# A two-layer hybrid backbone with product-key experts: 320 dense tokens in place of 384 in the first layer, the second context tile's gathers put last

## The chip, the cores and the metric

The kernel runs on one core of a Trainium2 chip. The time is the device time of one execution in microseconds, the median over several runs.

## The reference

Two layers over 512 latent tokens and 256 context tokens of width 1024. Each layer mixes tokens by three head groups and then sends every token through PEER, a product-key expert layer with 16384 one-neuron experts; 8 heads pick 16 experts each, 128 per token:

```python
hx = rmsnorm(x, norm1_g[l]) * (1.0 + sc1) + sh1
hc = rmsnorm(ctx, norm1_g[l]) * (1.0 + csc1) + csh1
yx, yc = token_mixer(hx, hc, need_ctx, ...)
x = x + g1 * yx
x = x + g2 * peer(rmsnorm(x, norm2_g[l]) * (1.0 + sc2) + sh2, ...)
# in peer:
act = gelu(einsum('td,thkd->thk', xb, u_tab[eid]))
return einsum('thk,thkd->td', gate * act, v_tab[eid])
```

`token_mixer` projects by `w_in` and runs a bidirectional RG-LRU (context first, its last states start the latents'), latent attention over context and latent keys, and a Hyena convolution (FFT) on the latents. The context is updated in layer 0 only; in layer 1 it still feeds the LRU and the attention. The output is the normalized latent stream.

## The kernel before, in words

Everything is in float32; where it pays, an operand is split into two float32r parts and multiplied in three passes (`mm`, `split`, `load_split`). The instructions are laid out by a tile framework at build time: under `prio(level)` a lower number goes first on each engine, and each engine then runs its queue in order. `schedule` (L173) sets the levels: the context's layer 0 first, the latents' layer 0 at 3, the dense experts at 3 (layer 1: 5), the gathers at 6, that is, wherever nothing else is ready.

Experts are computed in two ways. **Dense** (`peer_x`): T tokens go through all 16384 experts. 128 u-blocks of `peer_u` are split and multiplied with the tokens (`ublock`, tile `pst`), GELU goes into a ring of nA + nB slots (tiles `PA`, `PB`); `weights` builds each token's gates by comparing indices with an iota (`o`, `og`, matmuls `pwt`, L1231), eight tokens a unit, in three chunks of the 128 blocks, and multiplies them into the ring; `vblock` multiplies the slots with a v-block into PSUM (`dacc`). Every vn-th v-block is left unsplit and multiplied as plain float32. The last half tile of 64 tokens, where T has one, is always plain (L1254). The loop's order is written out: at step m the due weight units, v-block m, u-block m + R, R = nA + nB. Route (the top-16 choice) runs ahead of it beside the first nA u-blocks.

**Gathered** (`gtile_u`, `gtile_v`): for each of a tile's 128 choices an indirect DMA on the GpSimd queue (`rows_of`, L1089) fetches one table row per token, 128 rows of 4 KB, into one of five `grow` buffers; VectorE multiplies it with the tokens and sums (u, L1100) or adds it weighted to `acc` (v, L1113). A half tile (H) holds both halves of its choices side by side and needs 64 gathers of u and 64 of v. Full tiles are G, dense ones D.

Before the change, layer 0 gathers both context tiles (gc[0], gc[1]) and the latents' fourth tile (gx[3]): three times 128 of u and 128 of v, in the order gc[0] u and v, gc[1] u, gx[3] u and v, gc[1] v. Layer 1 gathers the fourth tile and half of the third.

`front` (L455 on) is the token mixer's first half: transposes (`transposed`), the `w_in` projections block by block (tile `pwin`), with `post` writing each to its place, through `upad` (padded by two memsets on GpSimd, L499 and L500 or their like) and `conv` where a convolution follows; then Hyena and the LRU (`lru`, matmuls `lpg`, L714). In layer 1 it runs with ctx=True: the blocks 9, 10, 11, 0, 1, 2 also project the context, for which `gtile_v` of gc[1] must have been written to `csd` and reloaded (`xr`, L424). The context's LRU comes ahead of the latents'. `back` holds the attention and the output projection. Pools on the left and right side are stacks: a pool opened later lies where a closed one lay, and its loads wait for it.

```python
for m in range(-nB, 128):
    for c, i in due.get(m, ()):
        weights(c, i, sp)
    if m >= 0:
        vblock(m, sp)
    if nA <= m + R < 128:
        ublock(m + R)
```

Of the kernel before, what the change touches and what calls it, by code (L numbers as in the profile page):

```python
# [9 lines left out]
F32 = mybir.dt.float32  # L10
F32R = mybir.dt.float32r
F16 = mybir.dt.float16
I32 = mybir.dt.int32
# [58 lines left out]
class Kern:  # L72
# [50 lines left out]
    def run(self):  # L123
        tc, nc, a = self.tc, self.nc, self.a
        with ExitStack() as es:
# [15 lines left out]
            nc.scalar.activation(self.scc, self.scc, AF.Silu)  # L141
            self.iota = pp.tile([128, 128], F32, name="iota")
            nc.gpsimd.iota(self.iota, pattern=[[1, 128]], base=0, channel_multiplier=0,
                           allow_small_or_imprecise_dtypes=True)
            self.iotah = pp.tile([128, 128], F16, name="iotah")
            nc.vector.tensor_copy(self.iotah, self.iota)
            self.ranks = pp.tile([128, 16, 8], F16, name="ranks")
            nc.vector.tensor_copy(self.ranks, self.iota[:, 0:16].unsqueeze(2).to_broadcast([128, 16, 8]))
            self.scaled = {}
# [23 lines left out]
    def schedule(self):  # L173
        a = self.a
        with ExitStack() as er:
# [27 lines left out]
            with self.prio(6):  # L203
                self.gtile_u(0, gc[0])
                self.gtile_v(0, 1, 0, gc[0])
                self.gtile_u(0, gc[1])
            with self.prio(3):
                gx, ex = self.peer_x(0, 384, 6, 32, 32, (36, 46, 46), ex)
            with self.prio(6):
                self.gtile_u(0, gx[3])  # L210
                self.gtile_v(0, 0, 3, gx[3])
                self.gtile_v(0, 1, 1, gc[1])
# [8 lines left out]
            with self.prio(5):  # L221
                gx, _ = self.peer_x(1, 320, 0, 32, 46, (44, 42, 42), ex)
            with self.prio(6):
# [230 lines left out]
    def front(self, es, ps, pr, l, s, low, side="left", split=True, ctx=False):  # L454
# [21 lines left out]
        with ExitStack() as es2:  # L476
            hp = es2.enter_context(self.pool("hyc" + tg, side=side))
            hc = [hp.tile([128, L], F32, name=f"hc_{i}") for i in range(6)]
            with self.pool("win" + tg, side=side) as sp:

                def post(st, L, j, p):
                    if j < 3:
                        u = sp.tile([128, LX + 3], F32, name="upad", bufs=2)
                        nc.gpsimd.memset(u[:, 0:2], 0.0)
                        nc.gpsimd.memset(u[:, L + 2:L + 3], 0.0)
                        nc.scalar.copy(u[:, 2:L + 2], p)
                        cw = [self.col(l, "lcw", i * 3 + j) for i in range(4)]
                        self.conv(st["xx"][j], u, L, cw, self.col(l, "lcb", j))
                    elif j < 6:
                        nc.scalar.activation(st["u1"][j - 3], p, AF.Gelu_apprx_tanh)  # L490
                    elif j < 9:
                        nc.scalar.copy(st["cq"][j - 6], p)
                    elif j < 11:
                        nc.scalar.copy(st["ckv"][j - 9], p)
                    elif j == 11:
                        nc.scalar.copy(st["kr"], p[:96])
                    else:
                        u = sp.tile([128, LX + 3], F32, name="upad", bufs=2)
                        nc.gpsimd.memset(u[:, 0:1], 0.0)  # L499
                        nc.gpsimd.memset(u[:, L + 1:L + 2], 0.0)  # L500
                        nc.scalar.copy(u[:, 1:L + 1], p)
                        cw = [self.col(l, "hcw", i * 6 + j - 12) for i in range(3)]
                        self.conv(hc[j - 12], u, L, cw, self.col(l, "hcb", j - 12))

                def parts(name, L):
                    return [sp.tile([128, KD, L], F32R if split else F32, name=f"{name}{i}") for i in range(1 + split)]

                hT = parts("hT", L)
                for _ in self.transposed(sp, ps, l, 0, s, range(L // 128), hT):
                    pass  # L510
                shared = (9, 10, 11, 0, 1, 2)
                order = (3, 4, 5, 6, 7, 8) + shared if ctx else (0, 1, 2, 9, 10, 11, 3, 4, 5, 6, 7, 8)
                for j in (12, 13, 14, 15, 16, 17) + order:
                    if ctx and j == shared[0]:
                        cT = parts("cT", LC)
                        for _ in self.transposed(sp, ps, l, 0, 1, range(2), cT):
                            pass
                    if split:
                        w = self.load_split(sp, "w_in", a["w_in"][l, j], bufs=3, parts=2)
                    else:  # L520
                        raw = sp.tile([128, KD, 128], F32, name="w_in", bufs=2)
                        nc.sync.dma_start(raw, a["w_in"][l, j])
                        w = [(raw[:, k, :],) for k in range(KD)]
                    for n, h, t in ((L, hT, st), (LC, cT, sc)) if ctx and j in shared else ((L, hT, st),):
                        p = ps.w("pwin")[:, :n]
                        for k in range(KD):
                            self.mm([p], [w[k]], [[x[:, k, :] for x in h]], k == 0, k == KD - 1)
                        post(t, n, j, p)
            with self.pool("nrm" + tg, side=side) as sp:
                self.rmsn(sp, ps, l, L, st["ckv"], "kvg", 256)  # L530
                self.rmsn(sp, ps, l, L, st["cq"], "qg", 384)
                with self.prio(low):
                    self.hyena(ps, l, s, hc, st["cat"], side)
        with self.prio(low), ExitStack() as ek:
            if ctx:
                kp = ek.enter_context(self.pool("kvc", side="right"))
                self.lru(pr, l, 1, sc, False, low - 1)
                self.mla(ps, ps, l, 1, sc, False, pool=kp)
            self.lru(pr, l, s, st, True, low - 1)
# [9 lines left out]
    def back(self, ps, pr, l, s, st, ex, mods=()):  # L549
# [6 lines left out]
        with self.pool(f"wo{l}{s}", side="right") as sp, ExitStack() as es2:  # L556
            wo = {}

            def load(pool, ks):

                for k in ks:
                    raw = pool.tile([128, D], F32, name="woraw" if l else f"wo{k}")
                    nc.sync.dma_start(raw, a["w_out"][l, k])
                    wo[k] = [raw]
                    if l:
                        wo[k] = [pool.tile([128, D], F32R, name=f"wo{n}{k}") for n in "hl"]
                        self.split(*wo[k], raw)
# [322 lines left out]
    def route(self, ps, l, s, kinds, hT=None, iT=None, i2n=None, side="left", done=None, fill=iter(())):  # L890
# [8 lines left out]
        with ExitStack() as es:  # L899
# [7 lines left out]
            with self.pool(f"rn{l}{s}", side=side) as sp:  # L907
                A2 = self.load_row(sp, l, 2, s, "A2")
                B2 = self.load_row(sp, l, 1, s, "B2")
                for i, x in enumerate(self.transposed(sp, ps, l, 1, s, range(nt), hT, rest)):  # L910
                    if kinds[i] == "D":
                        continue
                    outs[i] = h = gp.tile([128, D], F32, name="ghx", bufs=2)
                    for dst, src in ((LO, HI), (HI, HI)) if kinds[i] == "H" else ((ALL, ALL),):
                        nc.vector.tensor_mul(h[dst], x[src], A2[src])
                        nc.vector.tensor_add(h[dst], h[dst], B2[dst])
# [5 lines left out]
            sel = [self.sel_tiles(sp, i) for i in range(nt)]  # L922
            eid = {i: gp.tile([128, 128], I32, name="eid", bufs=3) for i in range(nt) if kinds[i] != "D"}
            for h in range(8):
# [167 lines left out]

    def gtile_u(self, l, routed):
        nc = self.nc
        hx, eid, gate, n = routed
        dot = self.gp.tile([128, 128], F32, name="dot")
        junk = self.gp.tile([128, D], F32, name="acc")
        for j in range(n):
            r = self.rows_of("peer_u", eid, j)
            nc.vector.scalar_tensor_tensor(junk, r, 1.0, hx, op0=ALU.mult, op1=ALU.mult, accum_out=dot[:, j:j + 1])  # L1100
        nc.scalar.activation(dot[:, :n], dot[:, :n], AF.Gelu_apprx_tanh)
        nc.vector.tensor_mul(gate[:, :n], gate[:, :n], dot[:, :n])

    def gtile_v(self, l, s, t, routed):
# [25 lines left out]
        if l == 0:  # L1130
            nc.sync.dma_start(self.sd[s][t], res)
            if s == 0:
                nc.sync.dma_start(self.res[0][:, t, :], self.sd[0][t])

# [15 lines left out]
    def peer_x(self, l, T, vn, nA, nB, widths, ex):  # L1150
# [11 lines left out]
        with ExitStack() as es:  # L1162
# [40 lines left out]
            def weights(c, i, sp):  # L1203
# [8 lines left out]
                nc.vector.tensor_tensor(  # L1212
                    paired(o1), paired(self.iotah[:, cuts[c]:cuts[c + 1]].unsqueeze(1)).to_broadcast(bc),
                    tk[:, 0].unsqueeze(2).to_broadcast(bc), op=ALU.is_equal)
# [6 lines left out]
                if i % 2 == 0:  # L1221
                    bc = [128, NC, 64, 2]
                    nc.vector.tensor_tensor(paired(o2), paired(self.iotah.unsqueeze(1)).to_broadcast(bc),
                                            tk[:, 1].unsqueeze(2).to_broadcast(bc), op=ALU.is_equal)
# [206 lines left out]
```

## Time and profile before

| what | value |
| --- | --- |
| median of the runs | 4282.57 us (4280.38 to 4297.57) |
| the profiled execution | 4280.5 us, span 4278.7 us |
| mean granted TensorE clock | 0.937 of 2.4 GHz |
| layer 0: route, dense experts | 905 to 1250, 1250 to 2475 us |
| layer 1: mixer, route, dense experts | 2475 to 2960, 2960 to 3260, 3260 to 4252 us |

The table's stages are read from the timeline; times are from the span's start. A row of the page or of a view names line, engine, operation and tile; xcount is the number of instructions. A busy PE is not PE at its peak, since matmuls overlap and their ends are modelled.

### The profile page before, as it was taken

Reading aid. Unit: us, or ns where it says so; the run is one execution under the profiler, and the core shown is the slowest. Engines: PE = TensorE matmul, PEld = TensorE weight load, DVE = VectorE, ACT = ScalarE, POOL = GpSimd, SP = SyncE. Lnnn points to the kernel's source line nnn. Section 1 sums busy time; section 2 is a strip of 40 time slices with the busy share of each in tenths; the row PEclk is TensorE's granted clock in tenths of the full one; section 3 lists DMA queues with packets and bytes.
Section 4 is the critical chain, followed back from the end, with each engine's and each line's share of the span. In section 5 each row is a group of like instructions: output and inputs, shape, how many; then the busy total and the mean of one; then the engine's idle time right before and its main releaser. Section 6 shows DMA issues by size and latency. Waiting matters only on the chain.

```text
span 4278.7 us, 63806 instructions
## 1 busy us (share of the span) xinstructions
PE 3732.9 (87%) x22530; PEld 2815.8 (66%) x22530; DVE 3506.5 (82%) x7435; ACT 1898.1 (44%) x3715; POOL 1524.6 (36%) x1225
## 2 busy tenths in 40 slices
PE   7887987968989989998868979887889999999997
PEld 3645544548878877877656657446888887776654
DVE  5746987889989988988898874754899998888988
ACT  4454342533247525622462233633325655555732
POOL 0000244652344563366426620000126345553243
PEclk7998997988999999999989989998999999999998
DMA  5554587885768897799879962252359888887697
GB/s 195 199 199 153 202 310 233 280 300 195 243 223 270 309 353 258 236 364 357 287 228 330 353 205 90 70 157 95 117 194 336 284 295 304 291 293 279 225 353 273
DMA packets 305154, 1062.90 MB, mean 248 GB/s; under 512 B 35468, under 2 KB 42336, under 8 KB 304834
## 3 DMA queue, kind: packets, MB, share of 16 engines
q0 software_dynamic: 165888, 604.05, 40.6%
q1 hardware_dynamic: 138946, 454.78, 30.5%
q8 instruction: 177, 2.90, 0.3%
q14 instruction: 143, 1.17, 0.1%
HBM read 1041.85 MB, written 16.84 MB: 247 GB/s over the span
## 4 chain that ended last, share of the span: by engine, by line
PE 33%; DMA 21%; DVE 17%; issue 16%; POOL 7%; ACT 5%; SPq 0%; POOLq 0%; DVEq 0%; ACTq 0%
PE pst L121 7%; POOL grow L1089 7%; DMA grow<-in_peer_u_dram,eid 6%; PE dacc L121 6%; DMA grow<-in_peer_v_dram,eid 5%; PE pwin L121 4%; DMA uv<-in_peer_ut_dram 4%; DMA uv<-in_peer_v_dram 4%; DVE uvl L114 3%; PE ppq L121 3%; DVE acc L1100 2%; DVE acc L1113 2%; DMA wmod<-in_w_mod_dram 2%; PE pwo L121 2%; PE fp L404 1%
## 5 line engine op out<-in xcount | busy, mean ns | idle before, releaser
L1089 POOL DMA_INDIRECT grow<-in_peer_u_dram,eid x576 | 754.0, 1309 | 1144.2 <-DVE acc L1100 562.0
L1089 POOL DMA_INDIRECT grow<-in_peer_v_dram,eid x576 | 762.7, 1324 | 767.3 <-DVE acc L1113 623.8
L121 PE MATMUL pst<-dhT,uvh 128*128 128x384 f32 (+1 forms) x4096 | 997.9, 328 | 0.0
L113 ACT CAST uvh<-uv 128x1024 fp32r<-128x1024 f32 x491 | 513.0, 1045 | 689.6 <-DMA uv<-in_peer_v_dram 414.2
L121 PE MATMUL pst<-dhT,uvl 128*128 128x384 f32 (+1 forms) x2048 | 695.1, 340 | 106.6 <-DVE uvl L114 75.0
L1113 DVE SCALAR_TENSOR_TENSOR acc<-grow,gate,acc 128x1024 f32<-128x1024 f32 x571 | 732.9, 1284 | 52.1 <-DMA grow<-in_peer_v_dram,eid 45.2
L1100 DVE SCALAR_TENSOR_TENSOR acc<-grow,ghx 128x1024 f32<-128x1024 f32 x576 | 704.6, 1223 | 66.7 <-DMA grow<-in_peer_u_dram,eid 61.3
L114 DVE TENSOR_TENSOR uvl<-uv,uvh 128x1024 fp32r<-128x1024 f32 x491 | 599.5, 1223 | 164.5 <-ACT uvh L113 160.5
L121 PEld LDWEIGHTS pst<-dhT,uvh 128*128 128x128 f32 x4096 | 729.8, 192 | 4.2 <-issue 2.2
L121 PEld LDWEIGHTS pst<-dhT,uvl 128*128 128x128 f32 x2048 | 394.3, 193 | 206.4 <-DVE uvl L114 154.8
L121 PE MATMUL dacc<-uvh,wl 128*128 128x512 f32 x1154 | 484.0, 420 | 38.5 <-DVE wl L114 22.3
L121 PE MATMUL dacc<-uvl,wh 128*128 128x512 f32 x1154 | 470.6, 408 | 20.4 <-DVE uvl L114 20.0
L121 PE MATMUL dacc<-uvh,wh 128*128 128x512 f32 x1154 | 466.3, 404 | 0.0
L1227 ACT ACTIVATE o<-iota,di2n 128x128 f16<-128x128 f32 x1056 | 325.5, 390 | 26.2 <-PE pwt L1231 26.0
L121 PEld LDWEIGHTS dacc<-uvh,wl 128*128 128x128 f32 x1154 | 222.3, 193 | 127.0 <-DVE wl L114 29.0
L121 PEld LDWEIGHTS dacc<-uvl,wh 128*128 128x128 f32 x1154 | 223.0, 193 | 79.2 <-DVE uvl L114 34.0
L121 PEld LDWEIGHTS dacc<-uvh,wh 128*128 128x128 f32 x1154 | 222.6, 193 | 48.8
L1231 PEld LDWEIGHTS <-o 128*128 128x128 f16 x4224 | 126.5, 97 | 113.3 <-DVE og L1217 33.4
L1231 PE MATMUL pwt<-og,o 128*128 128x46 f16 (+3 forms) x4224 | 152.5, 183 | 45.1 <-DVE og L1217 36.9
L1197 ACT ACTIVATE PA<-pst 128x384 f32<-128x384 f32 (+1 forms) x128 | 59.5, 464 | 281.7 <-PE pst L121 281.6
L1197 ACT ACTIVATE PB<-pst 128x384 f32<-128x384 f32 (+1 forms) x128 | 59.1, 462 | 222.7 <-PE pst L121 222.2
L254 POOL MEMSET rmod<- 128x512 f32 (+1 forms) x8 | 3.3, 416 | 422.8 <-DMA rows<-rmod 112.8
(398 smaller groups left out, 6122.2 us busy)
## 6 DMA issues: line engine op xcount, KB each, us to landing
uv<-in_peer_ut_dram SPq DMA_DIRECT2D x256, 512.0 KB
uv<-in_peer_v_dram SPq DMA_DIRECT2D x256, 512.0 KB
wmod<-in_w_mod_dram SPq DMA_DIRECT2D x96, 512.0 KB
wpq<-in_peer_wq_dram SPq DMA_DIRECT2D x48, 512.0 KB
w_in<-in_w_in_dram SPq DMA_DIRECT2D x72, 256.0 KB
w_in<-in_w_in_dram SPq DMA_DIRECT2D x18, 512.0 KB
grow<-in_peer_u_dram,eid POOLq DMA_INDIRECT x576, 6.5
grow<-in_peer_v_dram,eid POOLq DMA_INDIRECT x576, 6.7
```

The lines of the kernel that those rows point to most:

```text
L113: self.nc.scalar.copy(hi, src)
L114: self.nc.vector.tensor_tensor(lo, src, hi.bitcast(F32), op=ALU.subtract)
L121: self.nc.tensor.matmul(p, w[i], x[j], start=start and n == 0, stop=stop and n == len(passes) - 1)
L254: nc.gpsimd.memset(r, 0.0)
L404: self.nc.tensor.matmul(p, w, x, start=(i == 0), stop=(i == len(pairs) - 1))
L1089: self.nc.gpsimd.indirect_dma_start(out=r, out_offset=None, in_=self.a[table], in_offset=bass.IndirectOffsetOnAxis(ap=eid[:, j:j + 1], axi ...
L1100: nc.vector.scalar_tensor_tensor(junk, r, 1.0, hx, op0=ALU.mult, op1=ALU.mult, accum_out=dot[:, j:j + 1])
L1113: nc.vector.scalar_tensor_tensor(acc, r, w[:, j:j + 1], acc, op0=ALU.mult, op1=ALU.add)
L1197: nc.scalar.activation(slot(i), p, AF.Gelu_apprx_tanh)
L1227: nc.scalar.activation(o2[:, q], self.iota, AF.Abs, bias=i2n[:, t, k * NC + q:k * NC + q + 1])
L1231: nc.tensor.matmul(p[:, q, :], o2[:, q, :], og[:, g, q, :], start=(g == 0), stop=(g == 1))
```

## The change

In layer 0, 320 latent tokens are dense in place of 384: the third tile becomes H and is gathered too. Every second v-block is plain (vn 6 to 2), and the ring grows from 64 to 75 slots; layer 1's shrinks from 78 to 75. Of gc[1] only the first 32 u gathers stay ahead of the latents' tiles; the other 96 and its 128 v gathers come last. In layer 1's `front`, the context is projected in a `project` call of its own, with its own pool and a second load of six `w_in` blocks, behind Hyena in the order of the code. Smaller parts: the iota is kept in fp16 alone, `upad` is as long as its tile, `woraw` comes from another pool, `ghx` has three buffers, `heid` holds an H tile's indices, `gtile_v` writes the rows that it has.

```diff
             with self.prio(6):
                 self.gtile_u(0, gc[0])
                 self.gtile_v(0, 1, 0, gc[0])
-                self.gtile_u(0, gc[1])
+                self.gtile_u(0, gc[1], 0, 32)
             with self.prio(3):
-                gx, ex = self.peer_x(0, 384, 6, 32, 32, (36, 46, 46), ex)
+                gx, ex = self.peer_x(0, 320, 2, 32, 43, (42, 42, 44), ex)
             with self.prio(6):
-                self.gtile_u(0, gx[3])
-                self.gtile_v(0, 0, 3, gx[3])
+                for i in sorted(gx, reverse=True):
+                    self.gtile_u(0, gx[i])
+                    self.gtile_v(0, 0, i, gx[i])
+                self.gtile_u(0, gc[1], 32, 128)
                 self.gtile_v(0, 1, 1, gc[1])
...
-                gx, _ = self.peer_x(1, 320, 0, 32, 46, (44, 42, 42), ex)
+                gx, _ = self.peer_x(1, 320, 0, 32, 43, (44, 42, 42), ex)
...
-                shared = (9, 10, 11, 0, 1, 2)
-                order = (3, 4, 5, 6, 7, 8) + shared if ctx else (0, 1, 2, 9, 10, 11, 3, 4, 5, 6, 7, 8)
-                for j in (12, 13, 14, 15, 16, 17) + order:
-                    if ctx and j == shared[0]:
-                        cT = parts("cT", LC)
-                        for _ in self.transposed(sp, ps, l, 0, 1, range(2), cT):
-                            pass
+                for j in order:
                     if split:
-                        w = self.load_split(sp, "w_in", a["w_in"][l, j], bufs=3, parts=2)
+                        w = self.load_split(sp, "w_in", a["w_in"][l, j], bufs=bufs, parts=2)
...
-                    for n, h, t in ((L, hT, st), (LC, cT, sc)) if ctx and j in shared else ((L, hT, st),):
-                        p = ps.w("pwin")[:, :n]
-                        for k in range(KD):
-                            self.mm([p], [w[k]], [[x[:, k, :] for x in h]], k == 0, k == KD - 1)
-                        post(t, n, j, p)
+                    p = ps.w("pwin")[:, :L]
+                    for k in range(KD):
+                        self.mm([p], [w[k]], [[x[:, k, :] for x in hT]], k == 0, k == KD - 1)
+                    post(sp, st, L, j, p)
+
+            with self.pool("win" + tg, side=side) as sp:
+                project(sp, st, s, L, (12, 13, 14, 15, 16, 17, 0, 1, 2, 9, 10, 11, 3, 4, 5, 6, 7, 8), 3)
...
             if ctx:
+                with self.pool("winc", side=side) as sp:
+                    project(sp, sc, 1, LC, (0, 1, 2, 9, 10, 11), 3)
                 kp = ek.enter_context(self.pool("kvc", side="right"))
                 self.lru(pr, l, 1, sc, False, low - 1)
...
-    def gtile_u(self, l, routed):
+    def gtile_u(self, l, routed, j0=0, j1=None):
...
-        for j in range(n):
+        for j in range(j0, j1):
```

## Rows read from the trace of the kernel before

**Rows 1.** The page, part 1: busy us (share of span), instructions.

```profile
PE 3732.9 (87%) x22530; PEld 2815.8 (66%) x22530; DVE 3506.5 (82%) x7435; ACT 1898.1 (44%) x3715; POOL 1524.6 (36%) x1225
```

**Rows 2.** Windows by stage: length, busy (count), PE clock, DMA share, GB/s.

```profile
1250.00:2475.00 1225.00, 1100.81 (x6861) 895.98 (x6859) 1086.41 (x1683) 542.71 (x1053) 641.61 (x481) 0.96 0.87 305
2475.00:2707.00 232.00, 187.62 (x834) 146.39 (x834) 149.15 (x282) 98.20 (x200) 20.70 (x40) 0.89 0.37 125
...
3260.00:4252.00 992.00, 937.81 (x6345) 708.75 (x6344) 884.14 (x1370) 516.68 (x992) 450.04 (x330) 0.99 0.86 300
```

**Rows 3.** Windows within layer 0's dense stage; columns as before.

```profile
1440.00:1610.00 170.00, 157.28 (x724) 131.59 (x724) 144.16 (x218) 49.35 (x69) 111.73 (x82) 0.97 0.95 350
1610.00:1790.00 180.00, 171.80 (x1379) 143.22 (x1378) 164.10 (x332) 119.04 (x260) 61.45 (x48) 0.96 0.73 244
1790.00:2070.00 280.00, 256.37 (x1227) 210.87 (x1226) 239.47 (x278) 83.18 (x123) 174.70 (x131) 0.97 0.94 345
```

**Rows 4.** Waits of POOL, 1250 to 2475: us in total, times, longest.

```profile
POOL grow L1089 <- DVE acc L1113: 229.2, 121, 8.9
```

**Rows 5.** Groups by shape, DVE, 1250 to 2475: busy, mean ns.

```profile
L1113 DVE SCALAR_TENSOR_TENSOR acc<-grow,gate,acc 128x1024 f32<-128x1024 f32 x235 | 302.2, 1286 | 24.8 <-DMA grow<-in_peer_v_dram,eid 21.1
L1100 DVE SCALAR_TENSOR_TENSOR acc<-grow,ghx 128x1024 f32<-128x1024 f32 x244 | 298.3, 1223 | 24.0 <-DMA grow<-in_peer_u_dram,eid 21.3
L114 DVE TENSOR_TENSOR uvl<-uv,uvh 128x1024 fp32r<-128x1024 f32 x205 | 250.7, 1223 | 79.1 <-ACT uvh L113 78.3
```

**Rows 6.** Groups by shape, DVE, 3260 to 4252.

```profile
L114 DVE TENSOR_TENSOR wl<-PB,wh 128x256 fp32r<-128x256 f32 x64 | 26.9, 421 | 0.4 <-ACT wh L113 0.4
```

**Rows 7.** Timeline, layer 0's dense stage: start, length, engine, what.

```profile
1526.27 0.33 PE L121 MATMUL pst<-dhT,uvl 128*128 128x384 f32 x1
...
1526.79 0.33 PE L121 MATMUL pst<-dhT,uvl 128*128 128x384 f32 x1
...
2459.63 5.31 PE L121 MATMUL dacc<-uv,PB 128*128 128x512 f32 x12
```

**Rows 8.** Timeline of PE, layer 1's dense stage.

```profile
3562.72 0.57 PE L1231 MATMUL pwt<-og,o 128*128 128x42 f16 x16
...
3563.68 0.39 PE L121 MATMUL dacc<-uvh,wh 128*128 128x512 f32 x1
3563.91 0.39 PE L121 MATMUL dacc<-uvh,wl 128*128 128x512 f32 x1
...
3566.07 1.08 PE L1254 MATMUL dacc<-uv,PA 128*64 128x512 f32 x4
...
3568.05 0.31 PE L121 MATMUL pst<-dhT,uvl 128*128 128x320 f32 x1
...
3568.49 0.31 PE L121 MATMUL pst<-dhT,uvl 128*128 128x320 f32 x1
```

**Rows 9.** DMA, 2475 to 2525: a queue; issues, median us to landing.

```profile
q0 software_dynamic: 2546, 9.25, 55.0%
...
grow<-in_peer_v_dram,eid POOLq DMA_INDIRECT x16, 6.3
```

**Rows 10.** Window before the dense stage, L1089 alone (gathers).

```profile
1176.00:1250.00 74.00, 19.71 (x16) 0.88 0.48 160
```

**Rows 11.** Chain of waits, layer 1's projections: start, length, what.

```profile
2607.99 8.54 PE pwin L121 x48
...
2616.55 5.72 PE pwin L121 x24
```

**Rows 12.** Timeline of the front: last gather, reload, first LRU matmuls.

```profile
2517.06 1.28 DVE L1113 SCALAR_TENSOR_TENSOR acc<-grow,gate,acc 128x1024 f32<-128x1024 f32 x1
...
2526.55 0.42 SPq L424 DMA_DIRECT2D xr<-csd  x1
...
2661.52 1.03 PE L714 MATMUL lpg<-cxx,gw 128*128 128x256 f32 x4
...
2715.63 2.92 PE L714 MATMUL lpg<-xx,gw 128*128 128x512 f32 x6
```

More of the change, by code (lines that the diff above doesn't have):

```diff
@@ L141, in run @@
             nc.scalar.activation(self.scc, self.scc, AF.Silu)
[L142 to L146, printed above, removed]
-            self.ranks = pp.tile([128, 16, 8], F16, name="ranks")
-            nc.vector.tensor_copy(self.ranks, self.iota[:, 0:16].unsqueeze(2).to_broadcast([128, 16, 8]))
+            self.iota = pp.tile([128, 128], F16, name="iota")
+            self.ranks = pp.tile([128, 16, 8], F16, name="ranks")
+            with self.pool("iota") as sp:
+                iota = sp.tile([128, 128], F32, name="iota32")
+                nc.gpsimd.iota(iota, pattern=[[1, 128]], base=0, channel_multiplier=0,
+                               allow_small_or_imprecise_dtypes=True)
+                nc.vector.tensor_copy(self.iota, iota)
+                nc.vector.tensor_copy(self.ranks, iota[:, 0:16].unsqueeze(2).to_broadcast([128, 16, 8]))
             self.scaled = {}
@@ L478, in front @@
             hc = [hp.tile([128, L], F32, name=f"hc_{i}") for i in range(6)]
[L479 to L508, printed above, removed]
@@ new lines, in post @@
+            def post(sp, st, L, j, p):
+                if j < 3:
+                    u = sp.tile([128, L + 3], F32, name="upad", bufs=2)
+                    nc.gpsimd.memset(u[:, 0:2], 0.0)
+                    nc.gpsimd.memset(u[:, L + 2:L + 3], 0.0)
+                    nc.scalar.copy(u[:, 2:L + 2], p)
+                    cw = [self.col(l, "lcw", i * 3 + j) for i in range(4)]
+                    self.conv(st["xx"][j], u, L, cw, self.col(l, "lcb", j))
+                elif j < 6:
+                    nc.scalar.activation(st["u1"][j - 3], p, AF.Gelu_apprx_tanh)
+                elif j < 9:
+                    nc.scalar.copy(st["cq"][j - 6], p)
+                elif j < 11:
+                    nc.scalar.copy(st["ckv"][j - 9], p)
+                elif j == 11:
+                    nc.scalar.copy(st["kr"], p[:96])
+                else:
+                    u = sp.tile([128, L + 3], F32, name="upad", bufs=2)
+                    nc.gpsimd.memset(u[:, 0:1], 0.0)
+                    nc.gpsimd.memset(u[:, L + 1:L + 2], 0.0)
+                    nc.scalar.copy(u[:, 1:L + 1], p)
+                    cw = [self.col(l, "hcw", i * 6 + j - 12) for i in range(3)]
+                    self.conv(hc[j - 12], u, L, cw, self.col(l, "hcb", j - 12))
@@ L509, in front, with project @@
+            def project(sp, st, s, L, order, bufs):
+                hT = [sp.tile([128, KD, L], F32R if split else F32, name=f"hT{i}") for i in range(1 + split)]
                 for _ in self.transposed(sp, ps, l, 0, s, range(L // 128), hT):
                     pass
-                shared = (9, 10, 11, 0, 1, 2)
-                order = (3, 4, 5, 6, 7, 8) + shared if ctx else (0, 1, 2, 9, 10, 11, 3, 4, 5, 6, 7, 8)
-                for j in (12, 13, 14, 15, 16, 17) + order:
-                    if ctx and j == shared[0]:
-                        cT = parts("cT", LC)
-                        for _ in self.transposed(sp, ps, l, 0, 1, range(2), cT):
-                            pass
+                for j in order:
@@ L561, in load @@
                 for k in ks:
-                    raw = pool.tile([128, D], F32, name="woraw" if l else f"wo{k}")
+                    raw = sp.tile([128, D], F32, name="woraw") if l else pool.tile([128, D], F32, name=f"wo{k}")
                     nc.sync.dma_start(raw, a["w_out"][l, k])
@@ L912, in route @@
                         continue
-                    outs[i] = h = gp.tile([128, D], F32, name="ghx", bufs=2)
+                    outs[i] = h = gp.tile([128, D], F32, name="ghx", bufs=3)
                     for dst, src in ((LO, HI), (HI, HI)) if kinds[i] == "H" else ((ALL, ALL),):
@@ L922, in route @@
             sel = [self.sel_tiles(sp, i) for i in range(nt)]
-            eid = {i: gp.tile([128, 128], I32, name="eid", bufs=3) for i in range(nt) if kinds[i] != "D"}
+            eid = {i: gp.tile([128, 128], I32, name="eid", bufs=3) if kinds[i] == "G" else sp.tile([128, 128], I32, name="heid") for i in range(nt) if kinds[i] != "D"}
             for h in range(8):
@@ L1091, in rows_of @@
         return r
-    def gtile_u(self, l, routed):
+    def gtile_u(self, l, routed, j0=0, j1=None):
         nc = self.nc
         hx, eid, gate, n = routed
+        j1 = n if j1 is None else j1
         dot = self.gp.tile([128, 128], F32, name="dot")
         junk = self.gp.tile([128, D], F32, name="acc")
-        for j in range(n):
+        for j in range(j0, j1):
             r = self.rows_of("peer_u", eid, j)
             nc.vector.scalar_tensor_tensor(junk, r, 1.0, hx, op0=ALU.mult, op1=ALU.mult, accum_out=dot[:, j:j + 1])
-        nc.scalar.activation(dot[:, :n], dot[:, :n], AF.Gelu_apprx_tanh)
-        nc.vector.tensor_mul(gate[:, :n], gate[:, :n], dot[:, :n])
+        js = slice(j0, j1)
+        nc.scalar.activation(dot[:, js], dot[:, js], AF.Gelu_apprx_tanh)
+        nc.vector.tensor_mul(gate[:, js], gate[:, js], dot[:, js])
     def gtile_v(self, l, s, t, routed):
@@ L1130, in gtile_v @@
         if l == 0:
-            nc.sync.dma_start(self.sd[s][t], res)
+            nc.sync.dma_start(self.sd[s][t][rows], res[rows])
             if s == 0:
-                nc.sync.dma_start(self.res[0][:, t, :], self.sd[0][t])
+                nc.sync.dma_start(self.res[0][rows, t, :], self.sd[0][t][rows])
     def ended(self, sp, l, s, t, rows, y, old, res, fg=None):
@@ L1212, in weights @@
                 nc.vector.tensor_tensor(
-                    paired(o1), paired(self.iotah[:, cuts[c]:cuts[c + 1]].unsqueeze(1)).to_broadcast(bc),
+                    paired(o1), paired(self.iota[:, cuts[c]:cuts[c + 1]].unsqueeze(1)).to_broadcast(bc),
                     tk[:, 0].unsqueeze(2).to_broadcast(bc), op=ALU.is_equal)
@@ L1222, in weights @@
                     bc = [128, NC, 64, 2]
-                    nc.vector.tensor_tensor(paired(o2), paired(self.iotah.unsqueeze(1)).to_broadcast(bc),
+                    nc.vector.tensor_tensor(paired(o2), paired(self.iota.unsqueeze(1)).to_broadcast(bc),
                                             tk[:, 1].unsqueeze(2).to_broadcast(bc), op=ALU.is_equal)
```

## The prediction, made before the changed kernel ran

> **What bounds the kernel now.** The page's busy times come first: TensorE (PE) 87% of the span, VectorE (DVE) 82%, GpSimd (POOL) 36% [rows 1]; neither of the first two is full, so the answer must come from stages. The windows by stage [rows 2] show the first layer's dense experts from 1250 to 2475 us: PE 1100.8 of 1225, DVE 1086.4, DMA share 0.87 at 305 GB/s. Layer 1's dense stage, which already runs with 320 dense tokens, takes 992 us and looks alike (DMA 0.86, 300 GB/s). The front of layer 1, 2475 to 2707, is different: PE 187.6 of 232, DVE 149, DMA 0.37. So in the dense stages three resources run close to full together, and in the front DVE and DMA stand half idle.
>
> Inside the dense stage two kinds of stretch alternate [rows 3]: where few weight units are due (1440 to 1610, 1790 to 2070), the DMA share is 0.94 to 0.95 at 345 to 350 GB/s, with 82 gathers in 170 us of the first; where they are due (1610 to 1790), DVE is busy 164 of 180 us and only 48 gathers pass. What the gather queue waits for is mostly a `grow` buffer that DVE still holds, 229 us for L1113 [rows 4] and the like for L1100. A gather costs DVE 1.22 us and a short read of the accumulator behind it (u) or 1.29 us (v), so I count 1.29; a split of a weight block costs 1.22 us [rows 5]. Gathers are the lowest priority, so they take what the dense work leaves: 481 in 1225 us.
>
> The change takes dense work away and adds 128 gathers (half a tile, u and v), 896 in place of 768 in the first layer; beyond the first context tile's 256, which go first, 640 in place of 512. Context tile 1, whose last 224 gathers come last, must be finished before layer 1's context projection; that before the context LRU, and that before the latents' LRU. I therefore forecast one time: when the latents' LRU starts (2715.6 now [rows 12]). Everything behind it I take as unchanged, layer 1's own dense stage too: its ring shrinks from 78 to 75 u-blocks, so three u-blocks are made later by one v-step each; nothing to 8 us (one step, 992/128), taken as 0.
>
> **Part 1: the dense stage of layer 0.** PE: a group of three u-matmuls takes 0.52 us with 384 columns [rows 7] and 0.44 with 320 [rows 8]; 96 u-blocks x 8 groups x 0.085 = 65 us less. A split v-matmul takes 0.23 us (1.38 per full tile), a plain one 5.31/12 = 0.44 a record, two records to a matmul, so 1.77 a tile; a half tile costs 1.08 us [rows 7, 8]. Before: 107 split and 21 plain v-blocks of three tiles, 443 + 111 = 554 us. After (every second one plain, two and a half tiles): 64 x 3.84 + 64 x 4.62 = 541. Of the 144 weight units 24 go, at 0.57 us [rows 8]: 14 less. PE busy 1101 - 65 - 13 - 14 = 1009; from the other side, layer 1's 938 plus 64 x 0.78 for plain blocks = 988. I take 998. PE's idle time was 124 us here and 54 in layer 1 [rows 2]; there are fewer splits to wait for than here, but more gathers than there, so I take 76, a little under the middle: a stage of 1074 us, bounds 1052 and 1122, 151 us shorter.
>
> Gathers that fit: DVE's other work in layer 1 is 884 - 330 x 1.29 = 458 us [rows 2, 5]; with 64 fewer uvl and wl (1.22 and 0.42 us [rows 5, 6]) it is 353. At layer 1's DVE share of 0.89 that leaves (956 - 353)/1.29 = 467 gathers. DMA: 224 weight blocks of 0.52 MB pass in the stage; at the stage's own 305 GB/s 401 gathers fit beside them, at the 345 GB/s of a stretch with few weight units (1790 to 2070) [rows 3] 481. I take 440, the middle of these two, and less than DVE allows. The latents' 384 gathers go ahead of the context's tail, and with the 16 u gathers left of gc1's first 32 they are 400 of the 440, so the tiles just make the stage's end. 16 were issued before 1250 [rows 10]; the tail left is 640 - 16 - 440 = 184.
>
> **Part 2: the front.** The six shared blocks no longer project context beside the latents: 8.54 against 5.72 us [rows 11], 17 us less, so 232 becomes 215. Its other DVE work is 149 - 21 x 1.28 = 122 us, about 100 without the context's part. At a DVE share of 0.95, a little over the 0.91 of the fullest stretch in [rows 3], (204 - 100)/1.29 = 81 gathers fit. They slow the Hyena chain by up to one gather per hand-over, and the `upad` memsets now queue on POOL behind gathers that wait for a buffer; both cost nothing while the gather stream ends later than Hyena, and are next in line if it doesn't. The 103 gathers left run alone. In the run-out after 2475 the queue moved 9.25 MB in 50 us at a share of 55%, that is 336 GB/s, 1.56 us a gather; five buffers that land in 6.3 us and are held 1.29 give 1.52 [rows 9]. 103 x 1.56 = 161 us.
>
> The Trainium skill, "DMA: Bandwidth & Descriptors", section "Anatomy of one DMA — SWDGE (gpsimd) path", fits a gpsimd DMA at 2.0 us plus its bytes over 436 GB/s; by it a 512 KB gather would land in an estimated 3.2 us, five buffers would never be the limit, and the tail would run at DVE's pace, the second rival below. The trace's 6.3 us speaks against it.
>
> **Part 3: context behind Hyena.** From the last gather's DVE step to the tile's reload took 8.2 us (2518.3 to 2526.55 [rows 12]). Then a landing as a gather's, 6.3 [rows 9], and norm and transposes, estimated as long again: 13; three LRU projections, 3 x 2.82 = 8.5; convolution 2; the context LRU, estimated at half of the 46 us from its first matmul (2661.5) to the front's end at 2707, in which it took turns with Hyena: 23. Sum 55, bounds 45 and 80, the upper one since PE's clock may have fallen in the wait. The second load and split of six `w_in` blocks (3.1 MB, six gathers' worth, 9 us of DMA; 12 DVE pieces of half a uvl) hides in the wait; if the wait is gone, these 10 or so us are paid.
>
> At no cost: the fp16 iota, the third `ghx` buffer and the new pools of `upad`, `heid` and `woraw` (the same instructions, no new wait seen); the u part cut at 32 (two small operations more, under the gathers); the closing of one more tile (5 DVE pieces of 1.2 us, four gathers' worth, inside the bounds).
>
> **Sum.** 1250 + 1074 + 215 + 161 + 55 = 2755, 39 us later than 2715.6. The profiled execution took 4280.5 us; 4319.5 for it, and the median stands 2 us above: 4322. Break-even is a tail of 159 (465 gathers done by the stage's end); each gather more or less is 1.56 us. With 401 done, +100: 4384. With 467, -3: 4281. A stage length other than 1074 nearly cancels, as gathers go on in it.
>
> **Rivals.**
> 1. Faster: the dense stage fills the gaps that it has now, because the plain v-blocks leave DVE free just when the DMA queues have room. At the 350 GB/s of the best stretch throughout, 717 transfers, 493 of them gathers, pass (DVE at 0.95 would allow (1020 - 353)/1.29 = 517): the tail is 131, 50 x 1.56 = 78 us behind the 81 in the front, 44 us earlier: 4239. It decides from 465 gathers. For: DVE above 0.91 and DMA at 0.95 both occur [rows 3]. Against: never together, in neither layer. 0.30.
> 2. The tail at DVE's pace, 1.29 instead of 1.56: 103 x 1.29 = 133, so 11 later than now: 4294. For: in the dense stage POOL waited for DVE, hardly for a DMA [rows 4]. Against: [rows 9]. 0.15.
> 3. The dense stage holds layer 1's flow, 992/330 = 3.0 us a gather: 358 by its end, 42 latent gathers late (66 us, and layer 1 cannot begin), then a tail of 224 - 81 = 143 (223 us): 167 later, 4450. For: the twin stage shows just that. Against: its 128 split v-blocks took 105 us more of DVE. 0.10.
>
> **The numbers.** The forecast has 0.45; its own range is 4281 to 4384 (400 to 467 gathers), and about 0.08 of its chance lies within 0.5%. 0.5%, some 21 us, is about what a measurement of this kernel can tell from no change. Faster: rival 1 mostly, 0.30. Same: rival 2 and the low part of the forecast, 0.24. Slower: 0.46. The range of 8 in 10 takes in the forecast and most of rivals 1 and 2, and leaves out the third and the lowest part of the first: 4222 to 4390.
>
> **What would show it.** Right: layer 0's dense stage near 1074 us with about 440 gathers; gathers through the whole front and some 160 us on behind Hyena with PE idle; the latents' LRU near 2755. Wrong: DVE or DMA above 0.92 throughout the stage (rival 1); L1113 steps 1.3 us apart behind Hyena (rival 2); PE waiting for the latents' reload at the stage's end (rival 3); or a route, an LRU or a layer-1 dense stage of another length than now, which the sum takes as fixed.

## The result and the profile after

The changed kernel takes 4481.4 us (median of 4 runs, 4467.8 to 4486.1) against 4283.2 for the kernel before on the same chips: a ratio of 1.045 [1.0417, 1.0484]. The profiled execution took 4467.75 us, 187 more than the one of before. That lies 159 us above the forecast and beyond the range.

The windows by stage of the changed kernel (columns as in [rows 2]; the lines are layer 0's dense stage, the front to Hyena's end, the wait behind Hyena, the stretch from the latents' first LRU matmul to the end of the output projection, and layer 1's dense stage):

```profile
1250.00:2448.00 1198.00, 1056.58 (x6159) 687.35 (x6159) 954.63 (x1509) 448.10 (x891) 567.32 (x454) 0.97 0.86 302
2448.00:2676.00 228.00, 176.07 (x655) 126.55 (x653) 203.02 (x330) 63.36 (x124) 116.88 (x107) 0.85 0.83 284
2676.00:2871.00 195.00, 33.35 (x189) 28.54 (x190) 136.67 (x163) 43.32 (x91) 98.51 (x83) 0.57 0.69 239
2871.00:3121.00 250.00, 206.87 (x1103) 115.20 (x1101) 128.45 (x239) 99.30 (x176) 1.52 (x4) 0.89 0.32 104
3450.00:4442.00 992.00, 930.74 (x6272) 697.72 (x6272) 875.12 (x1358) 513.73 (x991) 427.30 (x323) 0.99 0.84 295
```

Against [rows 2]: layer 0's dense stage is 27 us shorter, where 151 were forecast, and now neither PE (0.88) nor VectorE (0.80) nor DMA (0.86) is near full. Layer 1's dense stage is within 6 us of what it was: 937 us from its first weight unit to its end at 4436, 931 before (the window above has the length of [rows 2] and runs 6 us past that end). Behind Hyena PE is busy for 33 of 195 us: 138 of them pass to the last gather (at 2814), 57 from there to the latents' LRU at 2871. That start, 155 us later than before, makes most of the 187; 25 more lie between it and the output projection (203 us, 178 before), 7 behind.

What had taken the dense stage is in the waits of SP, whose queue issues the weight loads. In the changed kernel (L1189 loads a block to be split, L1242 a plain one, L1255 is the half tile's matmul; us in total, times, longest), 1250 to 2448:

```profile
SPq L1242 <- PE dacc L1255: 194.7, 43, 10.1
SPq L1189 <- DVE uvl L114: 193.9, 75, 8.7
SPq L1189 <- PE dacc L1255: 154.2, 71, 5.6
```

And in the kernel before, 1250 to 2475:

```profile
SPq L1188 <- DVE uvl L114: 522.6, 152, 10.5
...
SPq L1188 <- PE dacc L121: 27.4, 18, 4.5
```

Before, a load waited for the subtraction that makes `uvl`, VectorE's last look at the raw block, a while before TensorE multiplies the parts. Now 349 us of the waits are for TensorE: the plain half tile reads the raw block itself, in most blocks at the end of their matmuls, and so does a plain block. The timeline of the changed kernel shows one such turn:

```profile
2210.64 1.07 PE L1255 MATMUL dacc<-uv,PA 128*64 128x512 f32 x2
...
2211.65 3.70 PE L121 MATMUL dacc<-uv,PA 128*128 128x512 f32 x8
2211.75 0.33 SPq L1189 DMA_DIRECT2D uv<-in_peer_v_dram  x1
...
2215.28 1.08 PE L1255 MATMUL dacc<-uv,PA 128*64 128x512 f32 x4
2216.40 0.33 SPq L1242 DMA_DIRECT2D uv<-in_peer_v_dram  x1
...
2219.47 1.04 ACT L113 CAST uvh<-uv 128x1024 fp32r<-128x1024 f32 x1 [8.31 <-DMA uv<-in_peer_v_dram]
2219.49 1.97 PE L1255 MATMUL dacc<-uv,PA 128*64 128x512 f32 x2 [3.13 <-DMA uv<-in_peer_v_dram]
2220.54 1.23 DVE L114 TENSOR_TENSOR uvl<-uv,uvh 128x1024 fp32r<-128x1024 f32 x1 [5.09 <-ACT uvh L113]
...
2221.69 2.60 DVE L1114 SCALAR_TENSOR_TENSOR acc<-grow,gate,acc 128x1024 f32<-128x1024 f32 x2
...
2223.23 1.86 POOL L1087 DMA_INDIRECT grow<-in_peer_v_dram,eid  x1 [5.73 <-DVE acc L1114]
```

The half tile's last matmul ends at 2211.71; 0.04 us later the load into its buffer starts. TensorE works on the other buffer until 2216.36 and then waits 3.1 us for the load. Behind that wait its granted clock is 0.50, the lower of its two levels (2219.49 to 2224.40; 1.00 from 2211.65 to 2216.36). The last lines are what the prediction had not seen: VectorE works through its queue in order, so while it waits 5.1 us for the cast of a block that has not landed, the gathers' steps behind wait too, and with them GpSimd for a `grow` buffer. The stall of the dense loop stalls the gathers. Over the stage, VectorE's waits for the cast are 133 us, where they were 78 [rows 5]:

```profile
L114 DVE TENSOR_TENSOR uvl<-uv,uvh 128x1024 fp32r<-128x1024 f32 x166 | 202.8, 1222 | 141.0 <-ACT uvh L113 132.7 <-issue 7.9
```

The same timeline shows a second cost of the half tile. Its two 512-column halves, issued together, run side by side: the four records at 2215.28 take 1.08 us. In the split blocks at 2210.64 and 2219.47 they are issued apart, and each takes as long as both: 1.07 us, or 1.97 at the lower clock. At 2219.49 the first half starts as the raw block lands, while the split parts are still being made. The half tile is torn like this in 31 of the 64 split blocks of the changed kernel. Its cost in the stage, in the changed kernel and in the one with three raw buffers (the first experiment), where it is whole in every block:

```profile
L1255 PE MATMUL dacc<-uv,PB 128*64 128x512 f32 x252 | 89.9, 630 | 8.3 <-DMA uv<-in_peer_v_dram 8.3
L1255 PE MATMUL dacc<-uv,PA 128*64 128x512 f32 x256 | 87.9, 643 | 9.0 <-DMA uv<-in_peer_v_dram 9.0
...
L1255 PE MATMUL dacc<-uv,PA 128*64 128x512 f32 x256 | 69.0, 618 | 0.0
L1255 PE MATMUL dacc<-uv,PB 128*64 128x512 f32 x256 | 69.0, 618 | 0.0
```

### The profile page after: what moved, and what is told of

Its sections match the earlier page's. It is cut to its first block, busy times and chain, and to the rows that moved or that the text cites. A ratio compares the mean times of both kernels' runs of the same rounds, so it can differ in the third digit from the quotient of the medians.

```text
span 4466.0 us, 62529 instructions
## 1 busy us (share of the span) xinstructions
PE 3693.4 (83%) x21824; PEld 2598.2 (58%) x21824; DVE 3569.7 (80%) x7462; ACT 1798.0 (40%) x3543; POOL 1640.2 (37%) x1353
## 4 chain that ended last, share of the span: by engine, by line
PE 35%; DMA 23%; DVE 17%; issue 13%; ACT 7%; POOL 5%; SPq 0%; DVEq 0%; POOLq 0%; ACTq 0%
PE dacc L121 8%; DMA uv<-in_peer_v_dram 8%; PE pst L121 7%; DMA uv<-in_peer_ut_dram 6%; POOL grow L1087 5%; DMA grow<-in_peer_u_dram,eid 3%; DMA grow<-in_peer_v_dram,eid 3%; PE dacc L1255 3%; DVE uvl L114 3%; PE ppq L121 3%; ACT uvh L113 2%; PE pwin L121 2%; DVE acc L1100 2%; PE pwo L121 2%; DVE acc L1114 2%
## 5 line engine op out<-in xcount | busy, mean ns | idle before, releaser
L121 PE MATMUL pst<-dhT,uvh 128*128 128x320 f32 x4096 | 932.6, 315 | 0.0
L1114 DVE SCALAR_TENSOR_TENSOR acc<-grow,gate,acc 128x1024 f32<-128x1024 f32 x634 | 812.4, 1281 | 75.5 <-DMA grow<-in_peer_v_dram,eid 66.4
L121 PE MATMUL pst<-dhT,uvl 128*128 128x320 f32 x2048 | 669.3, 327 | 104.4 <-DVE uvl L114 76.7
L121 PE MATMUL dacc<-uvh,wl 128*128 128x512 f32 x768 | 319.2, 424 | 52.4 <-ACT uvh L113 41.5
L121 PE MATMUL dacc<-uvl,wh 128*128 128x512 f32 x768 | 315.5, 411 | 22.3 <-DVE uvl L114 21.9
L121 PE MATMUL dacc<-uvh,wh 128*128 128x512 f32 x768 | 307.1, 400 | 0.0
L1228 ACT ACTIVATE o<-iota,di2n 128x128 f16<-128x128 f16 x960 | 296.5, 389 | 24.0 <-PE pwt L1232 20.4
L1255 PE MATMUL dacc<-uv,PA 128*64 128x512 f32 x512 | 163.2, 631 | 13.8 <-DMA uv<-in_peer_v_dram 12.9
L1255 PE MATMUL dacc<-uv,PB 128*64 128x512 f32 x512 | 164.6, 625 | 10.7 <-DMA uv<-in_peer_v_dram 10.7
L121 PE MATMUL pwin<-hT,w_inh 128*128 128x256 f32 (+1 forms) x672 | 165.8, 338 | 1.0 <-DVE hT L114 0.9
```

The costliest lines, as they stand in the source:

```text
L121: self.nc.tensor.matmul(p, w[i], x[j], start=start and n == 0, stop=stop and n == len(passes) - 1)
L1114: nc.vector.scalar_tensor_tensor(acc, r, w[:, j:j + 1], acc, op0=ALU.mult, op1=ALU.add)
L1228: nc.scalar.activation(o2[:, q], self.iota, AF.Abs, bias=i2n[:, t, k * NC + q:k * NC + q + 1])
L1255: nc.tensor.matmul(acc[nd][h * 64:(h + 1) * 64], slot(i)[:, nd * 128:T], raw[:, h * 512:(h + 1) * 512], start=(i == 0), stop=(i == 127))
```

## The experiments

Stage lengths below run from 1250 us to the first read of `dacc` at the stage's end, in the profiled execution of each kernel; ratios are to the kernel before on the same chip.

**A third raw buffer** (ring 75 to 71 slots; the same edit where a plain block is loaded):

```diff
-                raw = dn.tile([128, D], F32, name="uv", bufs=2 + l)
+                raw = dn.tile([128, D], F32, name="uv", bufs=3)
```

> The changed kernel with three raw `uv` buffers in layer 0's dense experts, as layer 1 has, instead of two (ring 75 to 71 slots to pay for it). Theory A (held buffers): with the half tile every v-block's raw buffer is held until its last plain matmul, and with vn=2 that of every second block through all its matmuls, so with two buffers the next load comes late. Then the dense stage falls from 1198 us to about 1080 (1040 to 1120), SP's waits for dacc L1255 ahead of a weight load (349 us in the changed kernel) fall below 120, the latents' LRU starts near 2800 instead of 2871, and the time is 4385 to 4415. Theory B (plain v-blocks themselves, their TensorE time): the stage stays above 1170, the time above 4440. Theory C (DMA bandwidth, gathers and weights together): the stage stays at 1180 to 1200 with the DMA share at 0.86, the time within 15 of 4467.

4415.2 us, 1.032 [1.0291, 1.0352]; its window of the stage:

```profile
1250.00:2372.00 1122.00, 1015.62 (x6278) 693.84 (x6276) 945.28 (x1494) 451.94 (x902) 568.77 (x442) 0.98 0.88 317
```

76 us less, with nearly as many gathers (442 against 453): B and C fall. The stage ends 2 us above A's band, and SP still waits 321 us for L1255, not under 120, so A's mechanism came only in part: the wait stays and costs less. A reason that fits is that with a third buffer another block is already there; VectorE's waits for the cast fall to 61 us. The half tile is whole here, 138 us of TensorE's time for 178, so the 76 us are not the buffer's wait alone.

**Fewer plain blocks** (vn 2 to 6, two buffers):

> The changed kernel with every sixth v-block plain, as before, instead of every second; two raw buffers. Theory A (held buffers): the half tile still holds the raw buffer in every block, so the stage stays at 1150 to 1200 us, the time 4430 to 4480. Theory B (plain blocks): 43 plain blocks fewer give the stage 1100 us or less and the time 4400 or less. Theory C (bandwidth): nothing changes, within 15 of 4467.

4533.3 us, 1.060 [1.055, 1.0645], above every band. The stage is as long as A said; with 43 more splits on VectorE only 402 gathers pass in it:

```profile
1250.00:2434.00 1184.00, 1065.74 (x6345) 723.20 (x6343) 958.99 (x1495) 506.05 (x979) 516.14 (x402) 0.97 0.82 283
```

**The same, with the half tile from `uvh`:**

```diff
-                                         raw[:, h * 512:(h + 1) * 512], start=(i == 0), stop=(i == 127))
+                                         (raw if l or len(v) == 1 else v[0].bitcast(F32))[:, h * 512:(h + 1) * 512],
+                                         start=(i == 0), stop=(i == 127))
```

> The vn=6 form of the changed kernel (stage 1184 us, 4533) in which the half tile of a split v-block multiplies with the block's upper part `uvh`, taken as plain float32, and not with the raw block: the same matmuls, but the raw buffer is free after the subtraction. It leaves out the lower part of v in the half tile. Theory A (held buffers): the stage falls to 1100 to 1140 us, SP's waits for dacc L1255 (283 us) fall below 60, the time to 4440 to 4490. Rival E (two buffers are too few under the gathers' load, whoever holds them): the stage stays at 1165 to 1190, the time within 20 of 4533.

4484.8 us. The stage is 111 us shorter than the one above, below A's band; SP's wait for L1255 ahead of a split block's load is 31 us where it was 233:

```profile
1250.00:2323.00 1073.00, 985.26 (x6331) 713.84 (x6332) 920.12 (x1460) 502.68 (x974) 482.86 (x377) 0.97 0.86 299
```

One reader of the raw buffer is gone in this pair, but two things went with it. The kernel above tears the half tile in 60 of its 107 split blocks, and L1255 takes 211 us of TensorE's time there and 145 here: that is 66 of the 111 us. So the pair shows what the raw reader costs, not what the held buffer alone costs. The time falls by 48 us alone, since 25 fewer gathers pass in the shorter stage and the tail has them.

**Three buffers and the half tile from `uvh`**, vn=2:

> The changed kernel with three raw buffers, and the half tile of a split block from its upper part (the lower part of v is left out there). Theory A (held buffers): with the half tile's hold gone too, the stage falls from 1122 to 1070 to 1100 us. If only plain blocks cost by now: 1110 to 1130. Time 4370 to 4415.

4377.8 us, 1.022 [1.0178, 1.0262], inside A's band, as the stage is:

```profile
1250.00:2337.00 1087.00, 999.02 (x6163) 683.74 (x6162) 938.47 (x1486) 444.94 (x890) 550.15 (x442) 0.97 0.92 328
```

So 1198 becomes 1122 and then 1087, 13 above the forecast's 1074, with the forecast's 440 gathers in it. The half tile is whole on both sides of the second step (138 us each), so its 35 us are the hold's. The DMA share rises to 0.92 and 328 GB/s: the changed kernel's 0.86 was no limit.

**No gathers:**

> The changed kernel with one gather of u and one of v for each tile that layer 0 gathers beside or behind its dense experts (the other 616 and their sums are left out). Theory A with the gathers' load (the held buffer hurts because a load takes long while gathers run): the stage falls from 1198 us to 1000 to 1050, near TensorE's busy time. Theory A alone (the hold matters without gathers too): 1110 to 1150. In both, the latents' LRU starts about 60 us behind Hyena's end, near 2540 in the first case (time near 4140), near 2640 in the second (4240).

4127.5 us, the stage 1018, the LRU 59 us behind Hyena:

```profile
1250.00:2268.00 1018.00, 997.87 (x6115) 664.26 (x6114) 418.11 (x774) 432.70 (x861) 1.01 (x1) 1.00 0.40 122
```

SP waits 356 us for the half tile here as well, and the half tile is torn here too (164 us), yet TensorE is idle for only 20 of 1018 us: without the gathers a late load still lands in time. So the hold costs because of the gathers. Whether by their transfers or by their steps on VectorE (busy 418 us here, 955 with them) this run does not say, for it takes out both.

**384 dense tokens again**, the order of the gathers and the late projection kept:

> The changed kernel with 384 dense tokens and every sixth v-block plain in layer 0, as before (ring 61): what is left of the change is the order of the gathers and the context's projection behind Hyena. Theories A, B and C alike (the loss lies in the 320-token dense stage): the stage takes 1225 us within 15, the last gather falls inside the front, the latents' LRU starts near 2735 (45 us behind Hyena's end for projection and context LRU), the time is 4285 to 4310. Theory D (the order and the late projection cost the most): LRU later than 2780, the time above 4350.

4351.7 us, 1.017 [1.0122, 1.0224]. A, B and C put too little here; D's time came, by 2 us, though its LRU (2780 or later) did not. The stage took 1249, not 1225 (its ring has 61 slots; whether that is why is not shown), no gather was late, and yet the LRU began at 2754, 38 us later than before, and the output projection another 25. Its windows (stage, front, LRU's wait, LRU to output projection):

```profile
1250.00:2499.00 1249.00, 1109.78 (x6908) 904.53 (x6906) 1110.48 (x1758) 551.34 (x1070) 676.60 (x494) 0.95 0.86 307
2499.00:2695.00 196.00, 159.58 (x646) 120.65 (x646) 115.95 (x213) 62.20 (x122) 7.91 (x27) 0.88 0.34 109
2695.00:2754.00 59.00, 33.05 (x188) 28.17 (x189) 31.62 (x77) 43.82 (x91) 0.13 (x2) 0.76 0.23 76
2754.00:2957.00 203.00, 160.19 (x911) 78.14 (x910) 114.58 (x226) 92.36 (x167) 1.25 (x4) 0.88 0.36 111
```

Projecting the context behind Hyena takes 37 us out of the front (196 against 233) and puts 51 behind it (LRU 59 us after Hyena's end, 8 before) and 25 more further on: a loss of 39 us by itself.

**`w_out` from GpSimd's queue**, for those 25 us:

```diff
-                    nc.sync.dma_start(raw, a["w_out"][l, k])
+                    (nc.gpsimd if l else nc.sync).dma_start(raw, a["w_out"][l, k])
```

> The changed kernel with layer 1's `w_out` rows loaded from GpSimd's queue, not SP's. Theory F (in the changed kernel the loads of wkvb, the rope tables and wqb stand on SP's queue behind a w_out load that waits 62 us for the LRU's space): they now come early, the stretch from the latents' first LRU matmul to the output projection falls from 203 us to about 178 as before, the time from about 4480 to 4455. Rival G (the stretch is long because TensorE's granted clock is 0.74 there, behind the wait): it stays at 195 to 205, the time too.

4483.7 us, a miss for F: the loads did come early and the stretch stayed, as G said. The timeline of this kernel; in the changed one wkvb was issued at 2910, behind a w_out load:

```profile
2875.50 0.33 SPq L779 DMA_DIRECT2D wkvb<-in_mla_wkvb_dram  x1
```

and its stretch from LRU to output projection:

```profile
2889.00:3094.00 205.00, 161.19 (x912) 78.31 (x910) 114.76 (x227) 92.61 (x167) 5.14 (x11) 0.87 0.33 101
```

But G's reason, the long wait ahead, is not it either: without gathers, LRU 59 us behind Hyena, the stretch is 205 us. In all the kernels with the late projection it holds 20 matmuls, 27 VectorE and 10 ScalarE instructions more than before, the context's norm, keys and values, which came ahead of the latents' LRU before; that is 10 us of TensorE. All of the 25 us lie ahead of the attention's first score, which comes 64 us behind the LRU's start in the changed kernel, 66 here and 39 before. Most of what is left is one wait of TensorE in it, first in the changed kernel (2871 to 2935), then here (2889 to 2956):

```profile
PE bps L766 <- DMA ropep<-in_ropep_dram: 13.3, 1, 13.3
...
PE bps L800 <- DVE bsw L768: 13.7, 1, 13.7
```

In the changed kernel the rope table lands late, as F said. Here it is there, but VectorE's step that needs it (L768) starts at 2936.25, behind the LRU's last steps and the split of a `w_out` row in VectorE's queue. The edit traded one wait for another of the same length.

**The kernel before with three raw buffers:**

> The kernel before with three raw `uv` buffers in layer 0 (ring 64 to 61 slots). Theory A: here no half tile holds a buffer; SP waits for DVE's subtraction (522 us), which is early against TensorE, so a third buffer gives little: stage 1195 to 1225 us, time 4250 to 4285. Theory C (bandwidth): nothing, 4275 to 4295.

4279.8 us, 1.0004 [0.9982, 1.0026]: as both theories have it; the stage, 1226, is 1 us above A's band. Without a half tile the buffer is worth nothing to the time; the gathers end at 2480 instead of 2518.

**The same, without plain v-blocks** (vn=0):

> The kernel before with three raw buffers in layer 0 (4280, its gathers done 38 us sooner than in the kernel before) and no plain v-blocks: TensorE has 21 x 3 x 0.39 = 25 us less, VectorE 21 x 1.78 = 37 us more. If the spare time of VectorE is worth something: the stage 1200 to 1215 us, the time 4255 to 4272. If VectorE's queue bounds the stage anyway: 1225 to 1250, 4280 to 4305.

4237.2 us, 0.9907 [0.9887, 0.9926], below both bands:

```profile
1250.00:2392.00 1142.00, 1046.24 (x6952) 898.63 (x6951) 1065.64 (x1729) 565.50 (x1093) 633.85 (x442) 0.97 0.86 309
```

**The kernel before, without plain v-blocks, two buffers:**

> The kernel before with no plain v-blocks, two raw buffers (ring 64). Theory H: most of the 84 us that the kernel with three buffers gained comes here too: stage 1140 to 1180 us, time 4235 to 4265. Rival J (the third buffer is needed for it): 1200 to 1225, 4270 to 4300.

4244.0 us, 0.9906 [0.9874, 0.9938], the stage 1154: theory H's bands. The buffer isn't needed for it. These two beat both kernels. The stage's gain is not all the plain blocks', though: 41 fewer gathers pass in it here, and 56 fewer in the pair with three buffers.

**The kernel before with every second block plain:**

> The kernel before with every second v-block plain (64 instead of 21), two raw buffers, 384 dense tokens and no half tile. Priced by TensorE alone: 43 x 3 x 0.39 = 50 us more of TensorE, 76 less of VectorE: the stage 1225 to 1275 us, time 4270 to 4330. Theory H at 4 us a block: 43 x 4 = 170 more, the stage 1350 to 1420, time 4400 to 4480.

4348.5 us, the stage 1305: between the bands. 80 us for 43 blocks is 1.9 each, more than TensorE's 1.17 even though VectorE had 76 us less to do, and though the gathers ended at 2451, so that the stage's last 104 us had none. The 21 blocks of the kernel before are worth 71 to 84 us of stage, 3.4 to 4.0 each, gathers not counted; of the time they are worth 40 us, 1.9 each.

**The changed kernel with three buffers and no plain blocks:**

> The changed kernel with three raw buffers and no plain v-blocks in layer 0, the form of layer 1's dense stage. Theory H (each plain block costs the loop far more than its 0.78 us of TensorE: 84 us for 21 of them in the kernel before with three buffers): the stage falls from 1122 us (three buffers, vn=2) to 1000 to 1050, layer 1's length, and the gathers keep layer 1's flow, 340 to 380 in the stage: time 4360 to 4410. Rival I (the 84 us were VectorE's, not the plain blocks'): the stage stays at 1100 to 1130, with fewer gathers, time above 4430.

4493.9 us. H's stage (1031) and flow (343 gathers), but not its time, which I had worked out wrong: 400 gathers belong to the latents' tiles or go ahead of them, so 57 were late, and the front, waiting for the tiles, took 326 us:

```profile
1250.00:2281.00 1031.00, 972.53 (x6538) 736.45 (x6536) 910.01 (x1478) 535.91 (x1030) 470.19 (x343) 0.98 0.84 294
2281.00:2607.00 326.00, 170.50 (x650) 123.80 (x646) 278.52 (x442) 63.67 (x124) 188.00 (x165) 0.75 0.86 294
```

## Why the prediction was wrong

The direction, slower, and the frame that the gather stream and then the latents' LRU decide, held; one step carried most of the miss.

- **Failed: "PE's idle time ... so I take 76 ...: a stage of 1074 us, bounds 1052 and 1122."** It was 1198, outside the bounds, with TensorE idle for 141 us (76 forecast) and busy for 1057 (998 forecast). The idle time was put between layer 0's and layer 1's, and the half tile's 1.08 us was read in layer 1. But layer 1, which has the half tile and the same width, has three raw buffers (`bufs=2 + l`); layer 0 has two, and had no half tile. The change brought a plain reader of the raw block into a stage with two buffers. The loads that wait for it and the half tile torn in two were not in the sum: the half tile alone took 178 us for 138, and the split passes 323 us where the repaired form takes 307, some of them at the lower clock behind a wait. Give back a buffer and the hold, and the stage is 1087 us, 999 busy and 88 idle. How the 111 us divide between the wait and the torn half tile with two buffers is not shown; with three, where nothing is torn, the hold is worth 35.
- **Failed with it: "A stage length other than 1074 nearly cancels, as gathers go on in it."** 124 us more brought 453 gathers instead of 440, so the number came out nearly right by a longer stage. The gathers stand in VectorE's queue behind the split that waits.
- Plain blocks priced by TensorE's time alone (0.78 us each): not settled. With three buffers, dropping 64 of them saves 91 us of stage (1122 to 1031), 1.4 each, but 99 gathers fewer pass in it, and the time is longer.
- Right: TensorE's work and the gathers by the stage's end once the raw reader is gone (999 us, 440 gathers, 181 left for 184), the gathers in the front (88 for 81), layer 1's dense stage (within 6 us). The chain behind the last gather is right in sum (57 for 55) by luck: to the context's first LRU matmul it took 24 us where the terms make 32, from there 33 where 23 was estimated.
- Mis-sized: the front, 228 us for 215. Without gathers it is 196 in the 384-token form, so they cost it about 30; no loss, as forecast, since the stream ended later. And the tail's pace: 81 gathers in 138 us are 1.70 each, not 1.56. In the tail (2690 to 2800) the gathers' queue alone kept the DMA engines at 89.9% and moved 34.25 MB in 110 us (columns as in [rows 9]):

```profile
q0 software_dynamic: 9407, 34.25, 89.9%
```

That is 311 GB/s, below the 336 taken from [rows 9], and slower than VectorE's pace of 1.29. By the fit of the Trainium skill, "DMA: Bandwidth & Descriptors", section "Anatomy of one DMA — SWDGE (gpsimd) path", a gather would land in an estimated 3.2 us, and the tail would have run at that pace; the trace does not agree.
- Failed: "Everything behind it I take as unchanged." 25 us came between LRU and output projection, from the context's work and the wait of 13 us shown above, and 7 behind.

On the LRU's start: 124 (stage) + 13 (front) - 23 (tail) + 2 (chain) = 116 us, the difference between the 39 forecast and the 155 measured. Rival 1 came within 12 of its 465 gathers, but in a stage 124 us longer and at 302 GB/s, not 350; rival 2's pace did not occur. Rival 3's time (4450) is near the measured one, but not by its mechanism: the latents' tiles were complete at 2326, 122 us before the stage's end. The mechanism did appear in the vn=0 form with three buffers.

With its stall repaired (1087 us) the kernel takes 4378 us, inside the range: about 104 of the 159 us by which the forecast was missed. The plan of the change fails even so: the ratio is 1.022, with 181 gathers left at the stage's end and 155 us from Hyena's end to the last of them. What remains open: how the raw reader's cost divides between held buffer and torn half tile, and what a plain block costs the loop apart from the gathers that it lets by.

## What to carry to other kernels

When a stage is forecast from a twin, compare the number of buffers behind each load as well as the shapes: who reads a buffer last decides when the next load starts, and a plain reader at the end of the matmuls can turn two buffers into one. Look too whether matmuls that ran side by side in the twin still stand side by side. Low-priority work in an in-order queue doesn't fill the stalls of the work ahead of it in that queue. Try an unsplit block's effect on the loop alone and do not go by its matmuls: dropping 21 of them from the kernel before was worth 0.9%.

## What was not expected of the hardware

The gathers alone moved less (311 GB/s at a share of 90%) than gathers and direct loads together (345 to 350 GB/s at 0.94 to 0.95 in [rows 3]). Two halves of a half tile issued together took 1.08 us, one alone 1.07.
